# Matmul with rotary embedding: TensorE turns one tile of x in each step of groups 1 to 3, instead of two in every second step

## The chip, the cores and the metric

The kernel runs on one core of a Trainium2 chip. The metric is the time of one execution on the device, in microseconds (us); lower is better. Five engines work side by side, each through its own list of instructions in order: PE (TensorE: matmuls, and the loading of their stationary operand, shown as PEld), DVE (VectorE), ACT (ScalarE), POOL (GpSimd) and SP (SyncE, which here only issues DMAs). They wait for each other on semaphores. Transfers between HBM and the on-chip memory run on 16 DMA engines.

## The reference

x has 16 batches of 512 rows of 768 values; the weight is 768 x 768; cos and sin are 512 x 64.

```python
y = np.matmul(x, weight).reshape(batch, seq, 12, 64)
y1, y2 = y[..., :32], y[..., 32:]
out1 = y1 * cos1 - y2 * sin1
out2 = y2 * cos2 + y1 * sin2
out = np.concatenate([out1, out2], axis=-1)      # 16 x 512 x 768, float32
```

So the work is one matmul of 8192 x 768 by 768 x 768, and behind it two products (with cos and with sin) and one sum for each value.

## The kernel before, in words

**Tiles, groups, pairs.** The 8192 rows of x are cut into 64 tiles of 128 rows. Four tiles make a group (`QB = 4`, 16 groups, 0 to 15), two tiles a pair. The main loop (L641 on) takes one tile per step: step i writes out the work of tile i, and of what runs ahead of it. There is no scheduler behind this: every engine's list is in the order in which this loop calls `do`, and `do` adds the waits that the reads and writes of named buffers need. Times and places of steps are thus all written by hand.

**The way of a tile.** (1) SP loads the tile into one of ten buffers `xs` (`load`, L201; `pump`, L491, sends the next load as soon as a cast has given a buffer up). (2) ACT casts it to 16 bit into one of five buffers `xc` (`cast`, L236; the copy itself is L185, a line that all casts and copies share). (3) PE turns it, since a matmul needs x with its 768 columns on the partitions: `turn_rows` (L256) issues 12 transposes of 64 rows each (L266), which write **both** halves of the one PSUM tile `pt`. (4) ACT copies `pt` into one of eight buffers `xt` (L185 again). `pt` has no second copy, so the next turn on PE has to wait until this copy is done. (5) PE multiplies with the weights (L362): six banks of PSUM, `py`, hold two pairs. The upper and lower 64 rows of the array run as two separate lines of matmuls (`walk`, `both`, L344 and L375); `both(upto)` writes out matmuls of both lines up to a count of columns, 4608 columns for a step, so `both(... + n * 1536)` is a third of a step. (6) DVE forms the two products out of `py` into `tq` or `w_raw` (L413), POOL adds them into `ov` (L430), and a DMA stores `ov` (L454), one tile per store and issued by ACT for most groups.

**Blocks.** In groups 5 to 14 the second pair of each group is not turned by PE. It is loaded in quarters (`load_quarter`, L220, issued by SP or, for even groups, by POOL) and turned by DVE (`turn_pair`, L294). PE therefore turns four tiles per group in groups 1 to 4 and two per group after that.

**Where turns and casts stand.** `turns(upto, 1)` turns the next tile if its number is below `upto`; `casts(upto, most)` casts up to `most` tiles below `upto`. Up to step 17 (`EVEN = 18`) a step turns tile i+2: an odd step after a third of its matmuls (L653), an even step behind its last matmul (L672). The two turns of a pair of steps have only that third of a step between them. Both casts stand at the end of the odd step (L678), behind both copies. From step 18 on, a step turns tile i+3 at its end and has one or two casts behind it (L672, L676); step 18 itself has two turns, one at its first third and one at its end. The stores of group 0 begin in step 12, and one store per step stands between the turn and the casts (L674).

Of the kernel before, what the change touches and what calls it, by code (L numbers as in the profile page):

```python
# [105 lines left out]
def kernel(  # L106
# [23 lines left out]
    QB = 4  # L130
# [3 lines left out]
    LAST = NG - 1  # L134
# [57 lines left out]
    def pair_of(i):  # L192
        return i // QB, (i % QB) // 2

    def is_block(i):
        return pair_of(i) in BLOCKS
# [77 lines left out]
    def cast_pair(gh, e="act"):  # L274
        k = xs[gh]
        c = ring("xd", NCP)
        xc[gh] = c
        do(e, copy(e, xd_b[c].rearrange("p (t j e) -> p t j e", t=NT, e=2),
                   xb_b[k].rearrange("p (j t e) -> p t j e", t=NT, e=2)),
           reads=[f"xb{k}q{q}" for q in range(NQ)], writes=[f"xd{c}"])  # L280
# [20 lines left out]
    def units(g):  # L301
        if g < LAST:
            cut = [2560] if g == LAST - 1 else []
            at = [0, 512, 1536, 2048] + cut + [3072]
            if g == 0:
                at = [*range(0, 3073, 512)]
            return [(c, z, py[:, c:z], [f"ps{b}" for b in range(c // 512, z // 512)],
                     "dve" if (g, c) == (LAST - 1, 2560) else "pool")
                    for c, z in zip(at, at[1:])]
        u = [(c, c + 512, py[:, c : c + 512], [f"ps{c // 512}"], "pool")  # L310
             for c in range(0, 2048, 512)]
        if g == LAST:
            for k, (home, bank) in enumerate([
                (py[:, 2048:2304], "ps4"), (py[:, 2560:2816], "ps5"),
                (pt_b[0][:, 0:256], "pt0"), (pt_b[1][:, 0:256], "pt1"),
            ]):
                c = 2048 + 256 * k
                u.append((c, c + 256, home, [bank], "pool" if k < 3 else "dve"))
        return u

    def pieces(g, s):

        out_, lo = [], s * H
        for c0, c1, ps, banks, _ in units(g):
            step = 512 if len(banks) > 1 else c1 - c0
            for k, b in enumerate(banks):
                a, z = max(lo, c0 + k * step), min(lo + H, c0 + (k + 1) * step)
                if a < z:
                    out_.append((a, z, ps[:, a - c0 : z - c0], b))
        return out_  # L330

    def mm_piece(i, piece, c, start, stop, tick):
        g, s = divmod(i, QB)
        a, z, ps, bank = piece
        get, key = xT[i]
        t, h = c
        do("pe", lambda eng: eng.matmul(  # L337
            ps, get(t, h), w_sb[:, t, h, a - s * H : z - s * H], start=start, stop=stop),
            reads=[key, f"w{t}{h}"], writes=[bank], tick=tick)
# [4 lines left out]
    def walk(pair, r):  # L344

        g, h = divmod(pair, 2)
        for bank in ((0, 1, 2) if r == 0 else (2, 0, 1)):
            opens = (r == 0) == (bank < 2)
            lo = h * 1536 + bank * 512
            parts = [(lo, lo + 512)] if bank != 1 else [(lo, lo + 256), (lo + 256, lo + 512)]  # L350
            for a, z in parts:
                i = g * QB + a // H
                for c in CHUNKS:
                    yield z - a, (g, i, a, z, r, c, opens,
                                  opens and (a, c) == (lo, CHUNKS[0]),
                                  c == CHUNKS[-1], z == lo + 512)
# [18 lines left out]
    def both(upto):  # L375

        while True:
            n = [(at[r], r) for r in (0, 1) if lines[r]]
            if not n or min(n)[0] >= upto:
                return  # L380
            r = min(n)[1]
            cols, what = lines[r].pop(0)
            at[r] += cols
            one(*what)
            g = what[0]
            for u in units(g):
                k = g, u[0]
                if k not in roped and {b for b in range(u[0] // 512, u[1] // 512)} <= ready.get(g, set()):
                    roped.add(k)
                    rope(g, u)  # L390
# [100 lines left out]
    def pump():  # L491

        while fetched[0] < len(fetch):
            j = fetch[fetched[0]]
            if isinstance(j, int):
                if xs_sent[0] - xs_used[0] >= NX:
                    return
                load(j)
                xs_sent[0] += 1
            else:  # L500
                if j[1] == 0:
                    if xb_sent[0] - xb_used[0] >= NB:
                        return
                    xb_sent[0] += 1
                load_quarter(*j)
            fetched[0] += 1
# [20 lines left out]
    def castx(i, e):  # L527
        cast(i, e)
        xs_used[0] += 1
# [43 lines left out]
    def casts(upto, most=NTILE):  # L573
        while state["cast"] < min(upto, NTILE) and most > 0:
            most -= 1
            i = state["cast"]
            state["cast"] += 1
            if not is_block(i):
                castx(i, "act")
            elif i % 2 == 0 and BLOCKS[pair_of(i)] == "sp":  # L580
                cast_pair(pair_of(i))
                xb_used[0] += 1
            pump()

    def turns(upto, most=NTILE):
        while state["turn"] < min(upto, NTILE) and most > 0:
            i = state["turn"]
            state["turn"] += 1
            if not is_block(i):
                most -= 1  # L590
                (turn_rows if rows_on[0] else turn)(i, "act")

    def bturns(upto):
        while state["bturn"] < len(pairs):
            gh = pairs[state["bturn"]]
            if gh[0] * QB + 2 * gh[1] >= upto:
                return
            turn_pair(gh)
            state["bturn"] += 1

    def pool_loads(upto):
        while state["pool"] < len(pool_pairs):
            gh = pool_pairs[state["pool"]]
            if gh[0] * QB + 2 * gh[1] >= upto:
                return
            for q in (0, 2, 1, 3):
                load_quarter(gh, q)
            state["pool"] += 1

    stores = {}  # L610
    for g in range(LAST):
        for s in range(QB) if g < LAST - 5 else (0, 2):
            if g < LAST - 5:
                i, n = 3 * QB + QB * g + s, 1
            elif g < LAST - 1:
                i, n = QB * (LAST - 3) + 3 + 2 * (g - LAST + 5) + s // 2, 2
            else:
                i, n = QB * (g + 1) + s, 2
# [1 line left out]
                (g, s * H, (s + n) * H, "act" if g < LAST - 2 else "sp"))  # L620

    C_AHEAD, T_AHEAD, B_AHEAD, P_AHEAD = 5, 3, 4, 20
    FIRST, EVEN, ROWS = QB + 2, 4 * QB + 2, QB * LAST - 2
    at[:] = [2 * 4608, 2 * 4608 + LAG]

    for i in (0, 1):
# [14 lines left out]
    for i in range(QB, NTILE):  # L641
        g, s = divmod(i, QB)
        us = units(g)
        done_to = (s + 1) * H
        rows_on[0] = QB <= i <= QB * LAST
        full = i < FIRST or i >= ROWS
        if not full:
            if s % 2 == 0:
                for r in range(2):
                    lines[r].extend(walk(i // 2, r))  # L650
            for n in range(1, 4):
                both((i - QB) * 4608 + n * 1536)
                if n == 1 and (i % 2 or i >= EVEN):  # L653
                    turns(i + T_AHEAD, 1)
        if i == ROWS:
            both(NTILE * 4608)
        for n, p in enumerate(pieces(g, s)) if full else ():
            a, z, _, bank = p
            if n == 1 and ROWS <= i < QB * LAST:
                turns(i + T_AHEAD, 1)  # L660
            for c in CHUNKS:
                if i < FIRST and (n, c) == (s, CHUNKS[3]):
                    turns(i + 2 + s, 1)
                mm_piece(i, p, c, c == CHUNKS[0], c == CHUNKS[-1],
                         tick=c == CHUNKS[-1])
            for u in us:
                if u[1] == z:
                    rope(g, u)
        bturns(i + B_AHEAD)
        if i == QB:  # L670
            casts(8)
        if i >= EVEN or i % 2 == 0:  # L672
            turns(i + (4 if i >= EVEN else 3), 1)
        for q in stores.get(i, ()):  # L674
            store(*q)
        if i >= EVEN:  # L676
            casts(i + 1 + C_AHEAD, 1 + i % 2)
        elif i % 2:  # L678
            casts(i + C_AHEAD, 2)
        pool_loads(i + P_AHEAD)  # L680
        if g == LAST:
            if s == 2:
                store(g, 0, H, "sp")
            if s == 3:
                store(g, H, 2 * H, "act")
# [44 lines left out]
```

## Time and profile before

| What | Value |
|---|---|
| median of 3 runs | 154.59 us (154.15 to 155.35) |
| profiled execution, own time | 154.0 us |
| its span in the trace | 152.2 us |
| granted TensorE clock | 0.991 of full |
| busy PE / DVE / ACT / POOL | 142.4 / 126.3 / 78.1 / 124.1 us |
| share of the chain that ended last: PE / ACT | 77% / 3% |
| moved by DMA | 51.28 MB, mean 337 GB/s |

How to read it: the span runs from the first to the last instruction of the profiled execution; 1.8 us of that execution lie outside of it. Busy time is a sum over the whole span, with different limits in different stretches. The chain follows the last instruction back to whatever released it, step by step, so a microsecond on the chain is a microsecond of the end. Groups 1 to 3 from step 6 on lie at about 22.5 to 49 us, and the last matmuls at 146 us.

### The profile page before, as it was taken

How to read it: one execution, taken by the hardware profiler on the slowest of the kernel's cores; microseconds unless marked ns; L12 is line 12 of the kernel's file. 1: busy time of each engine (PE TensorE's matmuls, PEld its weight loads, DVE VectorE, ACT ScalarE, POOL GpSimd, SP SyncE). 2: the span in 40 equal slices, each digit the busy share in tenths (PEclk: the TensorE clock that was granted, in tenths of full speed). 3: DMA queues.
4: the chain of work that ended last, by engine and by line, in shares of the span. 5: the costliest groups of instructions: out<-in, count | busy, mean ns of one | idle time of the engine just before them, and what ended most of it. 6: DMA issues, size and time to landing. Idle time of an engine off the chain costs nothing.

```text
span 152.2 us, 4356 instructions
## 1 busy us (share of the span) xinstructions
PE 142.4 (94%) x1907; PEld 103.0 (68%) x1907; DVE 126.3 (83%) x94; ACT 78.1 (51%) x91; POOL 124.1 (82%) x71
## 2 busy tenths in 40 slices
PE   6989999999999999999999999999999999999930
PEld 2345557676767777778887777787777778755620
DVE  0335996976768889899989998999989998999980
ACT  3464577768666892629161924375264826264000
POOL 1000797999669995999999999999996979999990
PEclk9999999999999999999999999999999999999996
DMA  4999999999999999999999999999998799996683
GB/s 128 400 394 402 404 401 371 252 268 308 278 296 401 327 338 356 352 406 340 344 349 392 357 333 358 370 402 368 359 356 314 305 383 385 391 375 244 252 315 103
DMA packets 27876, 51.28 MB, mean 337 GB/s; under 512 B 7505, under 2 KB 13393, under 8 KB 27857
## 3 DMA queue, kind: packets, MB, share of 16 engines
q1 hardware_dynamic: 14592, 27.92, 54.0%
q10 hardware_dynamic: 7824, 21.11, 35.5%
q0 software_dynamic: 5440, 1.97, 10.5%
q8 instruction: 15, 0.25, 0.6%
q14 instruction: 5, 0.03, 0.1%
HBM read 27.79 MB, written 25.17 MB: 348 GB/s over the span
## 4 chain that ended last, share of the span: by engine, by line
PE 77%; DVE 6%; DMA 4%; POOL 3%; ACT 3%; issue 2%; SPq 1%; POOLq 0%
PE py L362 64%; PE py L337 8%; PE pt L266 5%; DMA w_raw<-in_weight_dram 4%; POOL ov L430 3%; ACT xt L185 3%; DVE w_raw L413 2%; DVE tq L413 2%; SPq L205 1%; DVE ov L430 1%; POOLq L686 0%; PE pt L251 0%; DVE w_sb L185 0%; SPq L227 0%; SPq L725 0%
## 5 line engine op out<-in xcount | busy, mean ns | idle before, releaser
L430 POOL TENSOR_TENSOR ov<-tq 128x1536 f32<-128x1536 f32 (+3 forms) x33 | 77.8, 2378 | 4.6 <-DVE tq L413 4.4
L413 DVE TENSOR_TENSOR tq<-py,csn 128x1024 f32<-128x1024 f32 (+2 forms) x48 | 74.7, 1590 | 7.5 <-PE py L362 6.9
L362 PE MATMUL py<-w_sb,xt 64*128 64x256 f16 (+1 forms) x816 | 76.4, 323 | 0.0
L362 PEld LDWEIGHTS py<-w_sb,xt 64*128 64x128 f16 x816 | 52.7, 94 | 14.4 <-DVE tq L413 0.4
L185 ACT COPY xt<-pt 128x768 f16<-128x768 f16 x42 | 33.6, 801 | 54.6 <-PE pt L266 52.0
L362 PE MATMUL py<-w_sb,xp 64*128 64x512 f16 (+1 forms) x432 | 42.2, 323 | 0.0
L185 ACT CAST xc<-xs 128x768 f16<-128x768 f32 x43 | 37.3, 904 | 7.2 <-DMA xs<-in_x_dram 5.6
L413 DVE TENSOR_TENSOR w_raw<-py,csn 128x1024 f32<-128x1024 f32 (+1 forms) x21 | 35.1, 1672 | 3.9 <-PE py L362 3.5
L430 POOL TENSOR_TENSOR ov<-w_raw 128x1536 f32<-128x1536 f32 (+1 forms) x11 | 33.8, 3074 | 4.4 <-DVE w_raw L413 4.4
L362 PEld LDWEIGHTS py<-w_sb,xp 64*128 64x128 f16 x432 | 28.3, 94 | 7.5
L337 PE MATMUL py<-w_sb,xt 128*128 128x256 f16 (+1 forms) x114 | 20.2, 324 | 0.3
L266 PEld LDWEIGHTS pt<-ident,xc 64*128 64x128 f16 x468 | 13.6, 95 | 5.8 <-ACT xt L185 3.7
L337 PEld LDWEIGHTS py<-w_sb,xt 128*128 128x128 f16 x114 | 10.1, 98 | 8.1 <-DVE w_sb L185 1.5
L266 PE MATMUL pt<-ident,xc 64*128 64x64 f16 x468 | 13.7, 190 | 1.6 <-ACT xt L185 1.6
L185 POOL CAST xc<-xs 128x768 f16<-128x768 f32 x1 | 0.9, 884 | 14.6 <-PE py L337 14.6
L220 POOL DMA_DIRECT2D xh<-in_x_dram x20 | 11.7, 590 | 0.0
L185 ACT CAST xd<-xb 128x1536 f16<-128x1536 f32 x5 | 8.2, 1635 | 0.0
L185 DVE CAST w_sb<-w_raw 128x768 f16<-128x768 f32 x6 | 3.4, 558 | 3.4 <-DMA w_raw<-in_weight_dram 3.4
L294 DVE STREAM_TRANSPOSE xp<-xh 128x768 f32<-128x768 f32 x5 | 6.2, 1236 | 0.0
L514 PE MATMUL py<-tq 128*128 128x512 f16 x11 | 4.6, 583 | 1.4 <-DVE tq L458 1.4
L185 DVE COPY xt<-pt 128x768 f16<-128x768 f16 x2 | 1.1, 555 | 4.8 <-PE pt L251 4.8
L294 DVE STREAM_TRANSPOSE xp<-xd 128x768 f32<-128x768 f32 x5 | 4.8, 970 | 0.0
(21 smaller groups left out, 21.5 us busy)
## 6 DMA issues: line engine op xcount, KB each, us to landing
xs<-in_x_dram SPq DMA_DIRECT2D x44, 384.0 KB, 11.1
out_dram<-ov ACTq DMA_DIRECT2D x41, 384.0 KB, 7.6
out_dram<-ov ACTq DMA_DIRECT2D x6, 768.0 KB, 6.2
xb<-in_x_dram SPq DMA_DIRECT2D x20, 192.0 KB, 15.4
out_dram<-ov SPq DMA_DIRECT2D x4, 768.0 KB, 4.6
w_raw<-in_weight_dram SPq DMA_DIRECT2D x6, 384.0 KB, 6.6
xh<-in_x_dram POOLq DMA_DIRECT2D x20, 96.0 KB, 12.2
out_dram<-ov SPq DMA_DIRECT2D x1, 384.0 KB, 2.9
```

The source lines that it names most:

```text
L185: eng.copy(out=o, in_=i_) if e == "act" else eng.tensor_copy(out=o, in_=i_)
L205: do(e, lambda eng: eng.dma_start(out=xs_b[k], in_=x[b].rearrange("(p r) h -> r p h", r=SB)[r]), writes=[f"xs{k}"], dma=f"xs{k}")
L220: do(e, lambda eng: eng.dma_start(out=dst[ts(q, R)], in_=src[r, q]), writes=[f"{name}q{q}"], dma=name)
L266: do("pe", lambda eng: eng.transpose(pts[r][:, t, h, :], src[rows, t, h, :], ident[rows, rows]), reads=[f"xc{c}", "ident"], writes=[f"pt{r ...
L294: do("dve", lambda eng: eng.transpose(out=dst, in_=src), reads=rd, writes=[f"xp{z}"])
L337: do("pe", lambda eng: eng.matmul(ps, get(t, h), w_sb[:, t, h, a - s * H : z - s * H], start=start, stop=stop), reads=[key, f"w{t}{h}"], w ...
L362: do("pe", lambda eng: eng.matmul(py[:, a:z], get(t, h)[rows], w_sb[rows, t, h, a - s * H : z - s * H], start=start, stop=not opens and en ...
L413: do("dve", lambda eng: eng.tensor_tensor(out=tq.rearrange("p j (h d) -> p j h d", d=D), in0=ps.rearrange("p (h d) -> p h d", d=D) .unsque ...
L430: do(adder, lambda eng: eng.tensor_tensor(out=ov_b[o][:, ds(c0, w)].rearrange("p (h t d) -> p h t d", t=2, d=HD), in0=tq[:, 0].rearrange(" ...
L514: do("pe", lambda eng: eng.matmul(py[:, ts(b, 512)], cold[:, 0:P], cold, start=True, stop=warmed[0] < WARM - 6), reads=["tq0"], writes=[f" ...
```

## The change

It touches four places of the main loop. `EVEN` goes from 18 to 10, so the scheme that held from step 18 on now holds from step 10. In steps 6 to 9 every step, even or odd, turns tile i+2 after a third of its matmuls, and the turn at the end of even steps is left out (it stays in step 4). The casts of steps 4 to 9 are one per step (tile i+4), behind the turn's copy, instead of two in every odd step.

```diff
-    FIRST, EVEN, ROWS = QB + 2, 4 * QB + 2, QB * LAST - 2
+    FIRST, EVEN, ROWS = QB + 2, 2 * QB + 2, QB * LAST - 2
...
                 both((i - QB) * 4608 + n * 1536)
-                if n == 1 and (i % 2 or i >= EVEN):
+                if n == 1:
                     turns(i + T_AHEAD, 1)
...
-        if i >= EVEN or i % 2 == 0:
+        if i >= EVEN or i == QB:
             turns(i + (4 if i >= EVEN else 3), 1)
...
         if i >= EVEN:
             casts(i + 1 + C_AHEAD, 1 + i % 2)
-        elif i % 2:
-            casts(i + C_AHEAD, 2)
+        else:
+            casts(i + C_AHEAD, 1)
```

On PE the twelve turns of tiles 8 to 19 stay in their order and move among the same matmuls. Tiles 8, 10 and 12 go from the end of steps 6, 8 and 10 to the first third of the same steps; 9 and 11 stay where they are; 13 goes from the first third of step 11 to the end of step 10, and each tile from 14 to 20 likewise to the end of the step three before its own: 14 at the end of step 11, 15 at the end of step 12 and so on. On ACT the order becomes copy, cast, copy, cast, where it was copy, copy, cast, cast; from step 12 a store's issue stands behind each copy. The lists of DVE, POOL and SP have the same instructions in the same order as before. No instruction is added or left out.

## The prediction

> **What bounds the kernel now.** I read the page first, then the chain of waits in order of time between 22 and 52 us, then who waited for whom, then the busy time by stretch, and last POOL's timeline, to see whether a gain early on lives to the end.
>
> On the page, PE is the busiest engine, and the chain that ended last lies on it for 77%:
>
> ```profile
> PE 142.4 (94%) x1907; PEld 103.0 (68%) x1907; DVE 126.3 (83%) x94; ACT 78.1 (51%) x91; POOL 124.1 (82%) x71
> ...
> PE 77%; DVE 6%; DMA 4%; POOL 3%; ACT 3%; issue 2%; SPq 1%; POOLq 0%
> ```
>
> ACT's 3% is where to look. The chain in order of time (start, length, what), one pair of steps and then the place where the scheme of step 18 begins:
>
> ```profile
> 25.72 0.35 PE pt L266 x12
> 26.07 3.24 PE py L362 x30
> 29.31 0.22 PE pt L266 x12
> 29.54 0.02 issue
> 29.56 0.81 ACT xt L185
> 30.37 0.05 issue
> 30.41 0.35 PE pt L266 x12
> ...
> 49.18 0.35 PE pt L266 x12
> 49.53 1.96 PE py L362 x18
> 51.49 0.17 PE pt L266 x12
> 51.66 1.28 PE py L362 x12
> 52.95 0.19 PE pt L266 x12
> 53.13 5.85 PE py L362 x54
> ```
>
> The reader is to see a loop: turn, copy by ACT (0.81), next turn, and between the turns only a third of a step of matmuls, which ends before the copy does. It closes at 25.72, 30.41, 35.10, 39.80, 44.49 and 49.18: six times, 4.69 us apart. At 51.49 and 52.95, where two turns have 1.28 us of matmuls between them, the chain never leaves PE. Who waited for whom over the span (total us, times, longest) says the same:
>
> ```profile
> POOL ov L430 <- DVE tq L413: 4.4, 6, 1.5
> POOL ov L430 <- DVE w_raw L413: 4.4, 5, 1.5
> PEld pt L266 <- ACT xt L185: 3.7, 7, 0.5
> ...
> PE pt L266 <- ACT xt L185: 1.6, 6, 0.3
> ```
>
> PE stands idle 0.27 us six times; and each turn behind such a wait takes 0.35 of the chain, where one without takes 0.17 to 0.22.
>
> **The change, part by part.**
>
> *The six waits.* 54 + 18 matmul records of a group take 5.85 + 1.94 = 7.79 us further on in the chain (67.31 to 75.46), so a pair of steps has 3.895 us of matmuls. Now a pair takes 4.69 with two turns. After the change, two turns without a wait: 3.895 + 2 x 0.18 = 4.255. The difference is 0.435 us, and six of it are 2.6 us. Is every wait gone? In steps 6 to 10 the turns are a step apart, some 2.1 us; in step 10 two stand 1.28 us apart as at 51.49 and 52.95, where the copy (0.80) fits; from there again a step apart.
>
> *The price of a turn in its new place* is the one term the trace does not show as it will be. Nearest above: 0.35 for both turns, as behind a wait; a pair is then 4.595, and only 6 x 0.10 = 0.6 is gained. Nearest below: 0.17 for both, 2.7 gained. I take 0.18: the turn at 51.49 stands after the first third of an even step, exactly the new place, and took 0.17; that at 52.95 stands at a step's end and took 0.19. The 0.35 come only behind an idle PE; the wait alone, 6 x 0.27 = 1.6, is what I keep as the inner bound.
>
> *ACT.* Copies and casts are the same number. By stretch, one pair of steps, then a whole later group (length, then PE, PEld, DVE, ACT, POOL busy, clock, DMA share, GB/s):
>
> ```profile
> 30.41:35.10 4.69, 4.43 (x72) 3.31 (x72) 3.52 (x2) 3.21 (x4) 4.57 (x4) 1.00 1.08 276
> ...
> 67.31:75.46 8.15, 8.15 (x124) 6.46 (x121) 7.88 (x6) 4.74 (x5) 7.91 (x5) 1.00 1.13 352
> ```
>
> ACT has 3.21 us of work per pair, 1.04 less than 4.255. A copy now has one cast (0.91) ahead of it, not two; the cast begins right behind the copy before, so copy and cast are over some 1.7 us after it, ahead of the next turn at 2.1. If that cover went, a turn would wait for a late copy. The copy's nearest reader is the first matmul of the lower rows' line in the next pair, which begins with the odd tile: two thirds of a step (1.28 us) and `LAG`, 1024 of 4608 columns (0.43 us), after the turn; the copy is over 1.2 us after its turn begins (25.72 to 26.94), so some 0.5 us are spare there, as before. The first early cast, tile 8, goes to ACT's gap between the copies at 20.19 and 21.88, 0.89 us idle; I cost it at nothing.
>
> *DMAs that move.* From step 12 a store's issue (0.34 to 0.38 of ACT's queue) stands behind each copy and ahead of one cast instead of ahead of the next copy. The issues at 38.95 ran beside the copy of 38.94, and the group stored was added two groups earlier: nothing. Casts one tile earlier give buffers to SP one at a time; its list is unchanged. In this stretch ACT waits for no load (its only four waits for x, 5.6 us, end by 14.32), and the load that SP issued at 23.50, tile 18's, is cast at 45.60; with 9.9 us to landing for that one, some 12 are spare. POOL's list is unchanged, its four quarter loads (2.31 us) included.
>
> *Does it live to the end?* DVE has 3.52 of 4.255 per pair: not late. POOL is the tight one. Its adds in groups 1 to 4 (start, length, idle before):
>
> ```profile
> 31.40 7.03 POOL L430 TENSOR_TENSOR ov<-tq 128x1536 f32<-128x1536 f32 x2
> 39.68 3.46 POOL L430 TENSOR_TENSOR ov<-w_raw 128x1536 f32<-128x1536 f32 x1 [1.24 <-DVE w_raw L413]
> 44.30 3.46 POOL L430 TENSOR_TENSOR ov<-tq 128x1536 f32<-128x1536 f32 x1 [1.16 <-DVE tq L413]
> 47.70 2.31 POOL L220 DMA_DIRECT2D xh<-in_x_dram  x4
> 50.01 3.48 POOL L430 TENSOR_TENSOR ov<-tq 128x1536 f32<-128x1536 f32 x1
> 53.75 3.47 POOL L430 TENSOR_TENSOR ov<-w_raw 128x1536 f32<-128x1536 f32 x1 [0.25 <-DVE w_raw L413]
> 58.77 6.89 POOL L430 TENSOR_TENSOR ov<-tq 128x1536 f32<-128x1536 f32 x2 [1.54 <-DVE tq L413]
> ```
>
> From 31.40 to 58.77 it idles 1.24 + 1.16 + 0.25 + 1.54 = 4.2 us and is to lose 2.6 of it. Placed one behind the other, with DVE's ends earlier by 0.43 per pair passed, the add of 58.77 finds POOL free at 55.2 and its products at about 56.1: 0.9 us in hand. From there the order of before goes on, 2.6 us earlier; the chain lies on PE up to 132.15, and the tail of DVE and POOL behind it moves along.
>
> *Sum.* Profiled execution 154.0 - 2.6 = 151.4 us (span 149.6). That execution lies 0.59 under the median of the runs; the median to expect is 154.59 - 2.6 = **152.0 us**.
>
> **The rivals.**
>
> *POOL or DVE eats a part.* A later POOL group (8.15 us) idles 0.24; it can lose lateness only slowly. If adds or quarter loads took over 0.9 us more in all between 31 and 56, the rest would be late. For it: POOL is busy 4.0 of 4.0 us in many stretches. Against: its adds take 3.46 to 3.48 whether DVE is idle beside them or not, and at 116.05 and 123.94 it idles 1.52 and 0.98 again. Half the gain: 153.3 us.
>
> *The DMAs set the pace.* Their share is 1.04 to 1.23 in every stretch of groups 1 to 3. If loads came just in time, PE would wait for them instead, and nothing would be gained: 154.6. Against: no wait for a load after 14.32, and some 12 us spare. The Trainium skill, SBUF — State Buffer, section "A bandwidth-pool intuition that's wrong (but worth ruling out)", says that HBM is nearly always the bottleneck from end to end; by that rule this rival would hold, and the wait rows do not bear it out.
>
> *Slower: ACT becomes the loop.* A copy cannot pass the cast ahead of it in ACT's list; if that cast is late, the copy is, and the turn after it waits. It decides where copy, cast and what lies between exceed the 2.1 us between turns, that is, 0.4 us over the 1.7 above: a store issue (0.34) that does not run beside the copy, with a late load. Then twelve turns wait instead of six, at 0.435 each: 6 x 0.435 more than now, 157.2 us. Against: issue and copy overlap in the trace. The Trainium skill, TensorE: Matmul & The Clock Gate, Part 1, states that ScalarE's queue is strictly first in, first out; by it too no copy passes a late cast, and the starts in ACT's timeline, all in list order, agree.
>
> **How the numbers follow.** All six waits gone and kept to the end: 0.77, 152.0. A part eaten: 0.11, 153.3. DMAs: 0.05, 154.6. Slower: 0.07, 157.2. A measurement of this kernel can tell about 1% (1.5 us) from no change, so faster means under 153.05. That is the first case and a tenth of the second, 0.78; the same is the rest of the second and the third, 0.15; slower 0.07. Range: low 151.0, the profiled execution less 2.7, with 0.3 for scatter; high 153.7, which takes in waits gone at 1.6 us (153.0), half the gain (153.3) and the scatter of the runs above their median; left out are the DMA case, the slower one and little else. The likeliest case's own range is 151.0 to 153.0.
>
> **What would show it.** In the profile after: PE's waits for ACT's copy in the turns fall from 3.7 and 1.6 us to under 0.6 and nothing; pairs of steps 6 to 17 are 4.25 us apart; the chain has no ACT copy between 24 and 50 us; PE's turn costs 0.17 to 0.2 each; POOL's idle time before the add at (then) 56.2 is about 0.9; the last matmuls end at about 143.5 us. Wrong: turns of 0.35 without a wait, a new wait of turns for casts, POOL without idle time up to 60 us, or loads that ACT waits for.

## The result, and the profile after

| | before | after |
|---|---|---|
| median | 154.81 us (154.15 to 155.35, 4 runs) | 152.57 us (152.44 to 152.79, 4 runs) |
| ratio after / before | | 0.9859, 95% interval 0.9816 to 0.9902 |
| profiled execution, span | 154.0 us, 152.2 us | 152.5 us, 150.7 us |
| chain that ended last: PE / ACT | 77% / 3% | 80% / none shown |

The changed kernel is 2.24 us faster by the medians (154.81 - 152.57). The forecast was 2.6.

The chain in order of time, of the kernel after (start, length, what). First two steps that before held a copy by ACT, then one stretch that was not expected:

```profile
28.27 0.17 PE pt L266 x10
28.43 1.95 PE py L362 x18
30.38 0.15 PE pt L266 x9
30.54 0.03 PE py L362
30.57 0.03 PE pt L266
30.60 1.92 PE py L362 x17
32.52 0.17 PE pt L266 x10
...
34.19 1.09 PE py L362 x9
35.28 0.04 issue
35.32 1.07 PE py L362 x9
```

Turn, 1.95 us of matmuls, turn: the chain stays on PE, and no piece of ACT stands between 22 and 60 us. But at 35.28 there is a piece called "issue", which means that PE waited for nothing that the profile shows; the matmul before it started at 34.90, the next at 35.32, 0.42 us apart where 0.1 is usual. The waits on ACT's copy, of the kernel after between 22 and 52 us (total us, times, longest), are down to one, and the second row that stood there before is gone:

```profile
PEld pt L266 <- ACT xt L185: 0.4, 1, 0.4
```

Busy time by stretch, of the kernel after (length, then PE, PEld, DVE, ACT, POOL, clock, DMA share, GB/s), a pair of steps and a later group:

```profile
28.27:32.52 4.25, 4.25 (x84) 3.67 (x78) 3.52 (x3) 3.21 (x4) 4.23 (x6) 1.00 1.08 260
67.92:76.06 8.14, 8.14 (x124) 7.15 (x120) 7.83 (x6) 3.46 (x5) 7.81 (x3) 1.00 1.15 335
```

A pair takes 4.25 us, where it took 4.69; a later group takes what it took, 8.14 against 8.15. POOL's timeline, of the kernel after, around the add that had to be in hand:

```profile
39.66 3.48 POOL L430 TENSOR_TENSOR ov<-w_raw 128x1536 f32<-128x1536 f32 x1 [0.66 <-DVE w_raw L413]
43.84 3.47 POOL L430 TENSOR_TENSOR ov<-tq 128x1536 f32<-128x1536 f32 x1 [0.71 <-DVE tq L413]
...
52.98 3.48 POOL L430 TENSOR_TENSOR ov<-w_raw 128x1536 f32<-128x1536 f32 x1
57.17 6.88 POOL L430 TENSOR_TENSOR ov<-tq 128x1536 f32<-128x1536 f32 x2 [0.71 <-DVE tq L413]
```

POOL idles 0.71 us before the add of 57.17, so it is still waiting for work when the later groups begin, and passes the gain on.

**Where the time came from.** The executions start unevenly: DVE's first product (L413) begins at 15.14 us in the trace before and at 15.82 in the trace after, when the weights landed 0.7 us later; over all traces of this study it lies between 14.99 and 16.26. So spans of single traces are compared from that product on. From there to DVE's first block turn (L294, at the start of group 5's work) it is 40.39 us before (55.53 - 15.14) and 38.12 after (53.94 - 15.82). DVE's two rows, before and then after:

```profile
15.14 6.88 DVE L413 TENSOR_TENSOR tq<-py,csn 128x1024 f32<-128x1024 f32 x6
...
55.53 0.98 DVE L294 STREAM_TRANSPOSE xp<-xd 128x768 f32<-128x768 f32 x1
...
15.82 6.88 DVE L413 TENSOR_TENSOR tq<-py,csn 128x1024 f32<-128x1024 f32 x6
...
53.94 0.97 DVE L294 STREAM_TRANSPOSE xp<-xd 128x768 f32<-128x768 f32 x1
```

From the block turn to the start of DVE's last product it is 90.90 and 90.99. The whole gain lies in groups 1 to 4, 2.27 us, and next to nothing is given back later.

### The profile page after: what moved, and what is told of

It reads as the page before. It is cut to its first block, busy times and chain, and to the rows that moved or that the text cites. A ratio compares the mean times of both kernels' runs of the same rounds, so it can differ in the third digit from the quotient of the medians.

```text
span 150.7 us, 4352 instructions
## 1 busy us (share of the span) xinstructions
PE 141.9 (94%) x1907; PEld 112.3 (75%) x1907; DVE 126.3 (84%) x94; ACT 78.1 (52%) x91; POOL 124.0 (82%) x71
## 2 busy tenths in 40 slices
DMA packets 27875, 51.28 MB, mean 340 GB/s; under 512 B 7504, under 2 KB 13392, under 8 KB 27856
## 4 chain that ended last, share of the span: by engine, by line
PE 80%; DVE 6%; DMA 4%; POOL 3%; issue 2%; SPq 1%; POOLq 0%
PE py L362 67%; PE py L337 8%; PE pt L266 5%; DMA w_raw<-in_weight_dram 4%; POOL ov L430 3%; DVE w_raw L413 2%; DVE tq L413 2%; SPq L205 1%; DVE ov L430 1%; POOLq L686 0%; PE pt L251 0%; DVE w_sb L185 0%; SPq L227 0%; SPq L725 0%; SPq L116 0%
## 5 line engine op out<-in xcount | busy, mean ns | idle before, releaser
L413 DVE TENSOR_TENSOR tq<-py,csn 128x1024 f32<-128x1024 f32 (+2 forms) x48 | 74.7, 1590 | 5.6 <-PE py L362 5.0
L362 PE MATMUL py<-w_sb,xt 64*128 64x512 f16 (+1 forms) x816 | 77.3, 323 | 0.0
L362 PEld LDWEIGHTS py<-w_sb,xt 64*128 64x128 f16 x816 | 58.4, 94 | 9.1 <-issue 1.0
L362 PE MATMUL py<-w_sb,xp 64*128 64x512 f16 (+1 forms) x432 | 42.7, 323 | 0.0
L185 ACT CAST xc<-xs 128x768 f16<-128x768 f32 x43 | 37.9, 904 | 7.8 <-DMA xs<-in_x_dram 6.3
L413 DVE TENSOR_TENSOR w_raw<-py,csn 128x1024 f32<-128x1024 f32 (+1 forms) x21 | 35.1, 1672 | 3.7 <-PE py L362 3.5
L362 PEld LDWEIGHTS py<-w_sb,xp 64*128 64x128 f16 x432 | 31.6, 94 | 4.3
L266 PEld LDWEIGHTS pt<-ident,xc 64*128 64x128 f16 x468 | 15.1, 95 | 2.7 <-issue 1.1
L266 PE MATMUL pt<-ident,xc 64*128 64x64 f16 x468 | 15.5, 190 | 0.0
L294 DVE STREAM_TRANSPOSE xp<-xh 128x768 f32<-128x768 f32 x5 | 6.2, 1235 | 0.0
L294 DVE STREAM_TRANSPOSE xp<-xd 128x768 f32<-128x768 f32 x5 | 4.8, 968 | 0.0
```

Source lines behind the costliest of these rows:

```text
L185: eng.copy(out=o, in_=i_) if e == "act" else eng.tensor_copy(out=o, in_=i_)
L266: do("pe", lambda eng: eng.transpose(pts[r][:, t, h, :], src[rows, t, h, :], ident[rows, rows]), reads=[f"xc{c}", "ident"], writes=[f"pt{r ...
L294: do("dve", lambda eng: eng.transpose(out=dst, in_=src), reads=rd, writes=[f"xp{z}"])
L362: do("pe", lambda eng: eng.matmul(py[:, a:z], get(t, h)[rows], w_sb[rows, t, h, a - s * H : z - s * H], start=start, stop=not opens and en ...
L413: do("dve", lambda eng: eng.tensor_tensor(out=tq.rearrange("p j (h d) -> p j h d", d=D), in0=ps.rearrange("p (h d) -> p h d", d=D) .unsque ...
```

## The experiments

Both kernels write one turn into each step; what the title calls two in every second step are two turns with only a third of a step between them. Theory: PE lost time because the second of two close turns waited for ACT's copy of the first; turns a step apart lose nothing. Against it: that the casts' new places bring the gain; that the early start of the later scheme does; that the gain is lost later or to loads. And the question that the trace after raised: what the "issue" gap at 35.28 is.

Times are medians; ratios are to the kernel before on the same chip. "Stage" is the length just defined, from DVE's first product to its first block turn, in the profiled execution.

**e7 and e13: the changed kernel again.** No edit.

> The changed kernel once more, unaltered. My theory: the six waits of PE for ACT's copy are gone in every execution, so the ratio to the kernel before is 0.983 to 0.988, and turns lie 2.13 us apart. The open point is the one gap of 0.42 us between two matmuls at 34.90 us of the first trace, in which PE waited for nothing that the trace shows: if it is chance, it is missing here or lies elsewhere; if it belongs to the place in the program (the arrival of the next instructions), it lies at the same instruction again, about the 705th of PE, within 0.2 to 0.5 us.

> The changed kernel unaltered, beside which the next three are read: 152.4 to 153.6 us, ratio 0.984 to 0.990. In its profile the gap at PE's 705th instruction again, 0.4 us or more between two matmuls, ended 1.3 to 1.4 us after the end of the instruction packet before it.

Measured: 152.84 us, ratio 0.9884 (0.9848 to 0.9920); and 152.60 us, ratio 0.9855 (0.9818 to 0.9891). The gap came again, at the same instruction of PE, 0.71 us wide in e7 and 0.98 in e13. It is the 349th matmul in the record; the expectations call it PE's 705th instruction, counted from 0 with its weight loads and eight records of its sequencer. Both of e7's figures lie outside what was expected: its ratio, by a hair, above 0.988, and its gap above 0.5 us. The chain of e13:

```profile
34.09 1.09 PE py L362 x9
35.18 0.60 issue
35.79 1.07 PE py L362 x9
```

The same nine matmuls, then the gap, then the same nine as in the first trace: it belongs to the place in the program, and its width to the execution. Stages 38.41 and 38.67 us.

**e1: the turns alone**, against the kernel before.

```diff
-                if n == 1 and (i % 2 or i >= EVEN):
+                if n == 1:
...
-        if i >= EVEN or i % 2 == 0:
+        if i >= EVEN or i == QB:
```

> Only the turns move (steps 6 to 17 all turn at their first third; the scheme of step 18 stays at step 18; both casts stay at the end of odd steps). My theory (the copy of the first turn was late for the second): the six waits for the copy go, and the cast of the even tile, which stands right behind the odd tile's copy, is over about 2.0 us after that turn, 0.1 us ahead of the next turn; ratio 0.983 to 0.988. Rival (the casts must move too): the turns of even tiles now wait for their casts, 0.3 us or more in each pair, so that at least 1.8 us of the 2.2 us are given back; ratio 0.995 to 1.005.

Measured: 152.52 us, ratio 0.9871 (0.9836 to 0.9906), as the changed kernel. The weight loads of PE in this kernel show what leaving the casts behind costs:

```profile
24.10 0.23 PEld L266 LDWEIGHTS pt<-ident,xc 64*128 64x128 f16 x12 [0.63 <-ACT xc L185]
...
26.03 0.09 PEld L266 LDWEIGHTS pt<-ident,xc 64*128 64x128 f16 x1
...
28.31 0.27 PEld L266 LDWEIGHTS pt<-ident,xc 64*128 64x128 f16 x12 [0.17 <-ACT xc L185]
```

The first early turn waits 0.6 us for its cast; the later ones 0.2 or nothing, since the cast is over just in time. So the moved turns bring most of the gain, as the theory has it and against the rival. But the moved casts are worth something: the stage of e1 is 38.25 us, 0.55 above the 37.70 of the kernels below that have no gap, and some 0.4 of it (PE's 161st matmul starts 8.50 us after DVE's first product, against 8.12 in the kernel after) is lost at that first wait. The time does not show it, because PE, being later, finds only 0.13 us between the matmuls at the place of the gap.

**e2: the casts alone**, against the kernel before.

```diff
-        elif i % 2:
-            casts(i + C_AHEAD, 2)
+        else:
+            casts(i + C_AHEAD, 1)
```

> Only the casts move (one per step up to step 17); the turns stand as before, two with a third of a step between them. My theory: the loop turn, copy, turn stays closed, and the cast of 0.9 us now stands between the two copies, where it can only be harmless or make the second copy late, so nothing is gained: ratio 0.998 to 1.006, six waits of about 0.27 us on PE as before or longer. Rival (evenly spread casts are what helps): the time falls by 1 us or more, ratio under 0.994.

Measured: 154.77 us, ratio 1.0006 (0.9983 to 1.0029); stage 40.44 us. Who waited for whom in this kernel, 22 to 52 us:

```profile
PEld pt L266 <- ACT xt L185: 3.7, 7, 0.6
...
PE pt L266 <- ACT xt L185: 1.6, 6, 0.3
```

The six waits are all there. The rival falls.

**e3: the change without its first line** (`EVEN` stays 18), against the changed kernel.

```diff
-    FIRST, EVEN, ROWS = QB + 2, 2 * QB + 2, QB * LAST - 2
+    FIRST, EVEN, ROWS = QB + 2, 4 * QB + 2, QB * LAST - 2
```

> The change without its first line: turns at the first third of each step and one cast per step up to step 17, and the scheme of step 18 begins at step 18 as before. My theory: the place of the turn within a step does not matter, as long as they are a step apart: the same time as the changed kernel, ratio 0.983 to 0.988. Rival (the early start of the later scheme at step 10 brings part of it): only the two pairs of steps 6 to 9 gain, about 0.9 us, ratio about 0.994.

Measured: 153.34 us, ratio 0.9901 (0.9866 to 0.9936). This lies between the two expectations, and the trace says why. PE in this kernel:

```profile
34.79 0.59 PE L362 MATMUL py<-w_sb,xt 64*128 64x512 f16 x2
36.20 1.04 PE L362 MATMUL py<-w_sb,xt 64*128 64x512 f16 x11 [0.82 <-issue]
```

The gap is there again at the same instruction, 1.20 us from start to start, though another part of the step stands at that place here. The turns themselves lie 2.1 us apart up to step 17, as in the changed kernel. Taking the gap off, the stage is 38.93 - 1.20 = 37.7 us; the changed kernel's three traces come to 37.7 likewise (38.12 - 0.42, 38.41 - 0.71, 38.67 - 0.98), and the kernels below that have no gap take 37.69 to 37.71. The gap thus costs its whole width. So the place of the turns within the step does not matter, and the gap does.

**e4: a second buffer instead of other places.** The kernel before; steps 6 to 17 turn with six 128-row transposes into one half of `pt`, the halves in turn.

```diff
-        rows_on[0] = QB <= i <= QB * LAST
+        rows_on[0] = QB <= i <= QB * LAST and not FIRST <= i < EVEN
```

> The kernel before, with turns and casts where they were, but for steps 6 to 17 the turn of groups with a second buffer: six transposes of 128 rows into one half of pt, the halves in turn, so that a turn no longer waits for the copy of the one before. My theory (the missing second buffer is what the close turns cost): PE's six waits for the copy are gone at the old places too. A turn of six 128-row transposes takes 0.34 us in the first part of the trace, not 0.18, so a pair comes to 3.895 + 0.68 = 4.58 us against 4.69: 0.7 us gained, or nothing if the two lines of matmuls must be brought level each time (up to 0.1 us a turn). Ratio 0.994 to 1.006. Rival (PE does not wait for the copy but for something that lies with it): the six waits stay at about 0.27 us.

Measured: 156.72 us, ratio 1.0139 (1.0097 to 1.0182): a miss on the time. The chain of this kernel:

```profile
30.25 0.45 PE pt L251 x6
30.70 0.76 PE py L362 x7
31.46 0.44 PE pt L251 x6
31.90 3.35 PE py L362 x30
35.25 0.45 PE pt L251 x6
```

No copy by ACT stands in it, so the second buffer does end the waits at the old places; the theory's mechanism holds. But such a turn costs 0.45 us and not 0.34, and the matmuls of a pair 4.11 instead of 3.895: 5.0 us in all. That the two half-height lines have to be brought level around a full-height transpose is a possible cause of the latter, and was not measured by itself.

**e5, e8, e6: what makes the instructions late.** The trace records packets that carry instructions: 15 of them, 0.25 MB in the page's table of queues ("q8 instruction"), 16384 bytes each. The trace does not name their engine; they are taken for PE's, whose list has over 3800 records where no other engine has 150, and e4, with 144 fewer weight loads and matmuls, has 14 such packets. The second in the span ends before the gap in every trace that has one, and PE goes on 1.32 to 1.39 us after its end:

| kernel | packet, start to end | PE's 349th matmul | from the matmul before it | stage |
|---|---|---|---|---|
| before | 32.38 to 33.47 | 35.51 | no gap | 40.39 |
| e2 | 33.62 to 34.82 | 36.30 | no gap | 40.44 |
| after | 32.74 to 33.99 | 35.32 | 0.42 | 38.12 |
| e7 | 33.35 to 34.61 | 35.97 | 0.71 | 38.41 |
| e13 | 33.05 to 34.40 | 35.79 | 0.98 | 38.67 |
| e3 | 33.41 to 34.82 | 36.20 | 1.20 | 38.93 |
| e1 | 32.79 to 33.95 | 35.27 | 0.13 | 38.25 |
| e5 | 32.15 to 33.43 | 35.11 | no gap | 37.71 |
| e8 | 31.04 to 32.39 | 34.63 | no gap | 37.69 |
| e6 | 30.89 to 32.16 | 34.06 | no gap | 37.70 |

Theory: in this stretch the DMA engines are so full that the packet comes late. Three edits of the changed kernel take transfers out of it. e5 issues POOL's quarter loads four steps later, e8 issues SP's quarter loads one group later, e6 has 7 buffers for x instead of 10:

```diff
-    C_AHEAD, T_AHEAD, B_AHEAD, P_AHEAD = 5, 3, 4, 20
+    C_AHEAD, T_AHEAD, B_AHEAD, P_AHEAD = 5, 3, 4, 16
...
-        if soon and i >= max(2, soon[0][0] - 1) * QB:
+        if soon and i >= max(2, soon[0][0]) * QB:
...
-    NX, NB, NBH, NC, NCP, NXT, NXP, NOV = 10, 3, 3, 5, 2, 8, 4, 5
+    NX, NB, NBH, NC, NCP, NXT, NXP, NOV = 7, 3, 3, 5, 2, 8, 4, 5
```

> The changed kernel with POOL's quarter loads four steps later. Theory on the gap of PE at its 705th instruction (0.42, 0.71 and 1.20 us in three kernels): the packet with PE's next instructions comes late because the DMA engines are crowded at 28 to 34 us, and PE goes on 1.35 us after it is over; fewer transfers ahead of it bring it earlier by 0.5 us or more, the gap shrinks to its plain 0.1 us, and the time falls by 0.3 us against the changed kernel (ratio to the kernel before 0.983 to 0.986). Rival (the gap belongs to the place, whatever the DMA engines do): the packet still starts 16.9 to 17.5 us after DVE's first product and the gap stays at 0.3 us or more.

> The changed kernel with SP's quarter loads of blocks held back by one group (four tiles), POOL's where they are. By the theory that crowded DMA engines delay PE's instructions: small-packet loads leave the stretch 18 to 34 us, the packet starts earlier than 16.9 us after DVE's first product, the gap at PE's 705th instruction shrinks to about 0.1 us, and the time falls by 0.3 us against the changed kernel (ratio to the kernel before 0.983 to 0.986). Rival: packet and gap stay as they are.

> The changed kernel with 7 buffers for x instead of 10, so each load starts up to three tiles (6.4 us in this stretch) later. My theory (loads have some 12 us in hand, the DMA engines do not set the pace): no wait of ACT for a load behind 20 us, within 0.7% of the changed kernel; and as fewer loads are under way around 30 us, the instruction packet comes earlier and the gap at PE's 705th instruction shrinks. Rival (the loads come just in time): ACT waits for loads and the time rises by 2 us or more.

Measured: e8 151.84 us, ratio 0.9824 (0.9793 to 0.9855); e6 151.63 us, 0.9803 (0.9766 to 0.9840); both without the gap, their packets about a microsecond or more earlier from DVE's first product (15.5 and 15.9 us after it, against 16.9 to 17.3 in the changed kernel's traces). PE in e6 runs through the place:

```profile
33.12 0.38 PE L362 MATMUL py<-w_sb,xt 64*128 64x512 f16 x1
...
33.18 2.11 PE L362 MATMUL py<-w_sb,xt 64*128 64x256 f16 x24
```

e5 is a miss on the time: 152.90 us, ratio 0.9881 (0.9844 to 0.9917). Its profiled execution, 152.27 us, has no gap, but only just: 33.43 + 1.35 = 34.78 against 35.11. Three of its other five runs took 153.2 to 153.4 us. Whether the gap opened in those can't be read without their traces, and stays open.

**e10, e11, e12: controls and the better version.** e10 is the kernel before with 7 buffers; e11 joins e6 and e8; e12 has 6 buffers.

> The kernel before with 7 buffers for x instead of 10. My theory: in the kernel before, PE comes to its 705th instruction later than the packet allows (35.51 against 33.47 + 1.35 = 34.82 us), so there is no gap to win; the earlier packet is worth nothing here, and only a shorter start (first product of DVE earlier, 0.4 us at most) can show: 154.3 to 154.8 us. Rival (7 buffers help by themselves, whatever the turns): the same 0.9 to 1.2 us as in the changed kernel, 153.5 to 153.8 us.

> The changed kernel with 7 buffers for x and SP's quarter loads one group later. If both only bring the instruction packet ahead of the need, together they give no more than either: 151.5 to 151.9 us, no gap on PE. If early crowding costs at more places, another 0.2 to 0.4 us.

> The changed kernel with 6 buffers for x. My theory (some 12 us spare with 10 buffers, 2.13 us for each one less): about 3.5 us spare, so no lasting wait of ACT for loads in groups 1 to 3 and 151.4 to 151.9 us. Rival (the loads' lead is nearly used up): ACT waits for loads behind 20 us, the turns follow late, 152.5 us or more.

Measured: e10 154.65 us, ratio 0.9990 (0.9974 to 1.0007); e11 151.76 us, 0.9811 (0.9787 to 0.9836); e12 152.04 us, 0.9832 (0.9808 to 0.9856). In e10 the packet starts at 28.13 us, 4 us earlier than before, and the time stays: before the change, PE came to that place late enough, because it waited for ACT in six turns, three of them on the way. In e11 and e12 the packets start at 28.92 and 29.84, the gap is gone, and the stages are 37.7 us. The time of e12 lies a little above what was expected, 151.9 at most, and well under its rival's 152.5. In e12 ACT's last wait for a load, read in its timeline, is

```profile
15.43 0.88 ACT L185 CAST xc<-xs 128x768 f16<-128x768 f32 x1 [1.47 <-DMA xs<-in_x_dram]
```

so even with four buffers fewer no load is late in groups 1 to 3. The medians of e6, e11 and e8 lie within 0.21 us of each other and under those of both kernels; the changed kernel's were 152.57 to 152.84, and 152.60 (e13) in the runs made together with e11 and e12. The intervals of the ratios still touch (e13 from 0.9818, e11 up to 0.9836), so the size of this step is rough.

## Why the prediction was right, and which term it lacked

**The six waits: right, a little more than said.** Where there is no gap, the stage is 37.69 to 37.71 us in five traces (e5, e6, e8, e11, e12) against 40.39 and 40.44 (before, e2): 2.7 us, where 6 x 0.435 = 2.6 was put down. The chain has the pair at 4.25 us, as forecast. e2 shows that moving the casts alone leaves all six waits, e1 that moving the turns alone takes them, e4 that another buffer takes them too, at a price of its own.

**The price of a turn in its new place: right.** With all its pieces a turn takes 0.17 to 0.24 us of the chain after, and once 0.27 (at 36.39), where 0.18 was taken and 0.35 was the upper bound. The 0.35 goes with the idle PE in front: in e1 the one turn behind a long wait takes 0.35 again, the ones after it 0.17 or 0.18.

**ACT: right.** PE's waits for a copy in a turn fell to 0.4 us, one wait, over the whole span. The moved casts are needed once: in e1, without them, the first turn costs some 0.4 us, and behind it PE waits at most 0.2 us for a cast.

**Does it live to the end: right.** POOL had 0.71 us in hand where 0.9 was worked out, and from the first block turn to DVE's last product all traces take 90.9 to 91.0 us. This was the rival that POOL or DVE eats a part; it did not.

**The DMA rival: wrong as a rival, yet there was something in it.** Loads do not set the pace (e6, e12). The rule of the Trainium skill, SBUF — State Buffer, section "A bandwidth-pool intuition that's wrong (but worth ruling out)", that HBM is nearly always the bottleneck from end to end, is not borne out in this case: the change shortened the time with the same 51.28 MB moved, and of the changed kernel's variants those with fewer buffers for loads were the faster ones. But the crowded DMA engines did take something back, by a way the prediction did not have.

**The term that was missing.** The step that fell short is the sum, 154.59 - 2.6 = 152.0: it holds no term for the supply of PE's own instructions. In the part on DMAs that move, only loads, stores and quarter loads were gone through. The "issue" gap took 0.42, 0.71 and 0.98 us in the three traces of the changed kernel, 0.7 in the mean, and 2.7 - 0.7 = 2.0 us, against 2.24, 1.88 and 2.13 by the medians of the three comparisons. The median came within 0.6 us of the forecast because this term is small beside the six waits, not because it was foreseen. The cover that hid it is the very wait that was removed: before, PE came to that instruction at 35.51 us, 0.7 after the packet allowed it (33.47 + 1.35 = 34.82). That is the pattern of the prediction's DMA rival, a wait that takes the place of the one removed, but for PE's instructions and not for the loads of x.

**How firmly this is shown.** The gap stands at one instruction in four traces of two different programs; its end follows the packet's end by 1.33 to 1.39 us, and 1.32 in e1, where PE is held up by 0.1 us; kernels whose packet comes early enough have no gap, and the medians of e8, e6, e11 and e12 lie 0.5 to 1.2 us under those of the changed kernel; e10 has the early packet and no gain, since PE is late there anyway. That the packet itself comes late because loads are under way is shown by e6, e8, e11 and e12, which change nothing but loads, and by e10, where PE works as before and the packet still comes 4 us earlier; which of the loads hold it up was not tried, nor why it takes 1.35 us from the packet's end to the next matmul. The median of e5, 152.90 us, stays unexplained, since its one trace has no gap. Some of e6's lead may be chance: its profiled execution has the earliest start of all, 14.99 us.

**The slower rival** (each turn waiting for a copy behind a late cast) did not come: e2 has the same waits as before, 0.27 us and no longer, with a cast between the copies.

## What to carry to other kernels

When two uses of a single buffer stand close together and the next two far apart, spreading them evenly is worth the wait that stood between the close ones, and the price can be read from a place in the same trace where they already stand apart. Before the sum is closed, ask what else became due earlier when the wait goes: not only data, but also the engine's own instructions, which are transfers too. Loads that run further ahead than needed are not free while the DMA engines are full: in the changed kernel 7 buffers did better than 10, in the kernel before they made no difference.

## What the runs showed of the hardware

PE's instructions come in packets of 16384 bytes, 15 for the 3814 weight loads and matmuls in the record, so one for about 254 of them, through the same DMA engines as the data. The page of the kernel after lists them:

```profile
q8 instruction: 15, 0.25, 0.6%
```

At 0.6% of the engines' time they look harmless, yet one late packet stopped the busiest engine for up to 1.2 us; PE went on 1.32 to 1.39 us after the packet's end. The Trainium skill, Runtime: NRT & Kernel Launch, section "Instruction fetch mechanics", states that instructions are refilled in blocks of 256, or 16 KiB, which agrees with the packets here, and that this is mostly hidden, which the gaps of 0.42 to 1.20 us in four traces do not bear out for one packet of the 15, at a place with crowded DMA engines (a busy share of 1.08 over a pair of steps).
